# An RWKV-7 layer on one core: the first block's recurrence with the projections' pools kept open for its fillers, its outputs carried through DRAM

## The chip, the cores and the metric

The kernel runs on one core of a Trainium2 chip. The metric is the device time of one execution in microseconds, the median over several runs. A profile of one execution stands beside the times; its engines are named as in the profile: PE is TensorE (PEld its weight loads), DVE is VectorE, ACT is ScalarE, POOL is GpSimd, SP is SyncE, which issues most of the loads.

## What is computed

One layer on a sequence of 2048 tokens of width 1024, in float32: RMS norm, RWKV-7 time mixing with 16 heads of 64, residual, RMS norm, an MLP with squared ReLU and inner width 4096, residual, final RMS norm. The time mixing, cut to what matters here:

```python
xm = x[None] + xx[None] * mu[:, None, None, :]     # token shift, six mixings
rkv = jnp.einsum('nbsd,nde->nbse', xm[:3], w_rkv)  # r, k, v
g = jax.nn.sigmoid(xg @ g1) @ g2                   # gate, inner width 160
def rwkv7_step(state, inp):
    r_t, w_t, k_t, v_t, a_t, b_t = inp
    sa = jnp.einsum('bhvk,bhk->bhv', state, a_t)
    state = (state * w_t[:, :, None, :]
             + sa[..., None] * b_t[:, :, None, :]
             + v_t[..., None] * k_t[:, :, None, :])
    y = jnp.einsum('bhvk,bhk->bhv', state, r_t)
    return state, y
y = group_norm(y) * lnx_w + lnx_b                  # per head
bonus = jnp.sum(r_h * k_h * r_k, axis=-1, keepdims=True) * v_h
y = (y + bonus.reshape(b, s, d)) * g
return y.astype(x.dtype) @ w_o
```

## The kernel before

The sequence is cut into four blocks of 512 tokens. The kernel first runs the projections of all blocks, then the recurrence of block 0, then the rest, in which the output projection and the MLP of block i run while the recurrence of block i+1 is mixed in between. What one part leaves for a later one goes through DRAM: the scores' factors (`d_ar`, `d_bk`), the values `d_v`, the gates `d_g`, the bonus `d_bon` and the normed input `d_hn`.

**Projections.** `r_proj`, `k_proj` and an `epilogue` per block, written for a pool `am` on the right side of SBUF and a pool `ae` on the left; the PSUM pools are `psm` and `pse`. Values and gates are computed here for some blocks only: `v_proj` (L174) for block 0 and block 3, and `g_proj` (L193) for block 0. `g_proj` mixes eight tiles of the input (`mixed`, L143: a ScalarE scaling L157 and a VectorE multiply-add L158), which it reloads from `d_hn` (L170, two buffers `xs`), makes a small product L199 and a large one L209, a selection L211, a sigmoid, splits the gate and its weights into a high and a low part (L84, L85, L220, L228, L229), and runs eight output tiles of four products each (L90 to L92 and L234) whose results ScalarE copies into one of two store buffers `gs` (L236) and GpSimd stores to `d_g` (L237). `v_proj` without parts makes 16 products for each of 2 x 8 weight tiles (L186), and stores through two buffers as well (L190, L191). The eight mixed tiles of g0 take the place of `hn`, the input of the block.

**Recurrence of a block** (`stage_b`, L714): four windows of 128 tokens, each in four chunks of 32. `b_pre` (L558) loads the window's factors (Le, Lo, Bk, ecw, bonw) and makes four groups of score products (L577), which ScalarE copies and VectorE masks (L579 to L581). `b_solve` (L585) puts the scores' triangles into M by a transpose (L588) and solves them on VectorE by 30 steps of a multiply and an add (L595, L596); `b_inv` (L601) spreads the result out into `xbd` (L609). Then the four chunks (`b_chunk`, L611) run one after the other: a product pw, a copy to ws (L639), the product with the solved triangle pu (L642), copies to suv (L643 to L646), a state product pS and the new state. `b_y` (L665) makes the outputs y of the window, and `b_fin` (L676), for the two halves of the heads in turn, loads the values vb and the gates gb of the window (L688, L689), multiplies vb by the bonus (L691, L692), normalises y (L694 to L704), adds vb, multiplies by gb (L705, L706), transposes the result on TensorE (L710) and copies it to the tile `zt` in SBUF (L711), where the output projection of the block finds it. vb and gb have one buffer each.

**What sets the order.** The program is a chain of generators: a main one (projection steps) and a side one (recurrence steps), and after each main step a number of side steps is drawn. The instructions of each engine and of each DMA queue then run in the order that the tile framework's scheduler gives them, with semaphores for data and buffers. A tile pool is a region of SBUF or PSUM. A pool that opens in the space of another waits until what used that space is done, and the instruction that waits holds up what is queued behind it on its engine.

**Block 0's recurrence** has the stretch between the projections and the output projection for itself. Its first ten steps are drawn with nothing between; then `am` and `psm` are closed, pools `zq`, `fp` and `psf` are opened in their place, and as fillers on TensorE the values and gates that are still missing are run, in the order v1, g1, g2, g3, v2, with 1.9 side steps after each filler step (L744 to L762). `fp` has 16 tiles for mixed inputs and six for raw weights. Behind it all three pools are closed, and the pools `bp`, `cp` and `cps` of the last phase are opened in their space: `c_out` (L772) splits the tiles of z and makes the output projection po, `c_norm` the second norm, `c_up` and `c_down` the MLP, with the recurrence of the next block as side steps.

Of the kernel before, what the change touches and what calls it, by code (L numbers as in the profile page):

```python
# [9 lines left out]
F32 = mybir.dt.float32  # L10
# [7 lines left out]
P = 128  # L18
# [21 lines left out]
def trunk(ctx: ExitStack, tc, xt, vecs, lnw, lnb, wr, wk, wv, w1a1, w2, a2,  # L40
# [21 lines left out]

    d_hn = [dram.tile([P, KT, TB + 1], F32, tag=f"d_hn{i}", name=f"d_hn{i}") for i in range(NB)]
# [79 lines left out]
    def mixed(e, hk, vmu, name, parts=True):  # L143

        res = []
        for k in range(KT):
# [3 lines left out]
            elif e.xw:  # L150
                x32 = e.sb.tile([P, TB], F32, tag="x32", name=f"{name}_{k}", bufs=e.xw)
            else:

                if k == 0:
                    xall = e.sb.tile([P, KT, TB + 1], F32, tag="hn", name=f"{name}_all")
                x32 = xall[:, k, 0:TB]
# [17 lines left out]
    def v_proj(e, i, hk, parts=True):  # L174

        xs_ = mixed(e, hk, V_MV, f"xv{i}", parts)
# [16 lines left out]
    def g_proj(e, i, hk):  # L193
        xs_ = mixed(e, hk, V_MG, f"xg{i}", False)
# [311 lines left out]
    run(g_proj(e, 0, reload_hn(e, 0, "g")))  # L506
# [169 lines left out]
    def b_fin(w, r, bp, ps, cfg):  # L676
# [3 lines left out]
        if wd == 0:  # L680

            zts[i] = [(bp if i % 2 else zq).tile([P, 4, TB], F32, tag=f"zh{i % 2}{q}", name=f"zt{i}_{q}") for q in range(2)]
        zt = zts[i]
        for par, y in enumerate(r.y):
# [26 lines left out]
            nc.scalar.copy(zt[par][:, :, wd * WIN:wd * WIN + WIN], pz)  # L711
# [30 lines left out]
    for _ in range(EARLY):  # L742
        next(side)
    pm_.close()  # L744
    zq = ctx.enter_context(tc.tile_pool(name="zq", bufs=1, side="right"))
    with ExitStack() as pf:
        fp = pf.enter_context(tc.tile_pool(name="fp", bufs=1, side="right"))
        psf = pf.enter_context(tc.tile_pool(name="psf", bufs=1, space=PSUM, side="right"))
        FILL = (("v", 1), ("g", 1), ("g", 2), ("g", 3), ("v", 2))
        VS = (None, False, False)  # L750
        e = Env(fp, psf, wb=2, wr=4 if True in VS else 6, xb=8 if True in VS else 1, tb=2, mm=4, xw=8 if True in VS else 16, xs=2)
        BU = 1.9
        acc = 0.0
        for f, i in FILL:
            for _ in (v_proj if f == "v" else g_proj)(e, i, reload_hn(e, i, f), *((VS[i],) if f == "v" else ())):
                acc += BU
                while acc >= 1.0:
                    acc -= 1.0
                    next(side, None)
        for _ in side:  # L760
            pass
    p0.close()  # L762
# [9 lines left out]
    def c_out(i):  # L772

        t0 = i * TB
        zt = zts[i]
        zs = [split(e, zt[k // 4][:, k % 4, :], f"z{i}_{k}") for k in range(KT)]
# [174 lines left out]
```

## Time and profile before

| | |
|---|---|
| time, median of 3 runs | 2986.18 us (2983.82 to 2986.3) |
| the profiled execution | 2978.28 us, span 2976.6 us, mean granted clock 0.978 |
| DMA, mean over the span | 126 GB/s, 373.92 MB |
| last value projection ends | 669.3 us |
| first product with a solved triangle | 735.27 us |
| last y of block 0 starts | 958.12 us |
| first product of the output projection | 1000.0 us |

A row of the trace gives start and length in us, engine, line, operation, output tile <- input tiles, shape, type and the count of instructions that were put together; brackets at its end give the idle time of the engine ahead of it and what ended that. "SPq" is SyncE's queue of DMA issues, "POOLq" that of GpSimd. Rows that group (`by form`) give the busy sum, the mean ns of one, and the idle time ahead of all of them. Matmul ends are modelled by the profiler, so that a sequence of matmuls in one row may overlap the next row a little. The granted clock stands as a share of 2.4 GHz.

### The profile page before, as it was taken

What the parts mean: (1) busy time and instruction counts of PE and PEld (TensorE: products, weight loads), DVE (VectorE), ACT (ScalarE), POOL (GpSimd) and SP (SyncE); (2) the same over time, 40 slices, a digit from 0 to 9 for tenths busy, and PEclk for the clock granted to TensorE, in tenths of its full rate; (3) what the DMA queues carried; (4) which work ended last, traced back from release to release, by engine and by line L of the source; (5) the groups of instructions that cost most, each with busy time, mean ns of one, the idle gap of its engine ahead of it and who ended that gap; (6) DMA issues with size and microseconds to landing.
All of it is one profiled execution on the core that took longest, in us unless ns stands there. A gap on an engine that the chain in (4) does not pass through costs nothing.

```text
span 2976.6 us, 50052 instructions
## 1 busy us (share of the span) xinstructions
PE 2819.1 (95%) x19144; PEld 2129.0 (72%) x19144; DVE 2050.7 (69%) x3858; ACT 1440.7 (48%) x2639; POOL 297.5 (10%) x348
## 2 busy tenths in 40 slices
PE   8999999987989989999998999999899999999998
PEld 5766667754555668777777777778777777878886
DVE  5688888866886577667568767866876786544443
ACT  5667666643474353443534444354445435343342
POOL 0102020131110110000012000001200000110000
PEclk9999999998999999999999999999999999999999
DMA  4444454566563533424343433343333332333332
GB/s 132 152 152 160 152 185 163 169 204 196 152 203 111 155 88 101 114 83 119 98 143 103 112 112 96 110 119 119 110 111 114 93 112 82 113 121 96 92 99 78
DMA packets 192543, 373.92 MB, mean 126 GB/s; under 512 B 41136, under 2 KB 41712, under 8 KB 187696
## 3 DMA queue, kind: packets, MB, share of 16 engines
q1 hardware_dynamic: 175216, 305.49, 34.8%
q0 software_dynamic: 17088, 65.24, 5.8%
q8 instruction: 150, 2.46, 0.4%
q14 instruction: 89, 0.73, 0.1%
HBM read 303.32 MB, written 67.32 MB: 125 GB/s over the span
## 4 chain that ended last, share of the span: by engine, by line
PE 67%; DVE 15%; issue 6%; ACT 5%; DMA 5%; POOL 2%; SPq 0%; ACTq 0%; DVEq 0%; POOLq 0%
PE pd L92 6%; PE pd L91 6%; PE pd L90 6%; PE pu L91 6%; PE pu L90 6%; PE pu L92 5%; DVE tmp L595 2%; DVE M L596 2%; PE pk L90 2%; PE pk L91 2%; PE pk L92 2%; PE po L90 2%; PE po L92 2%; PE po L91 2%; PE pr L90 2%
## 5 line engine op out<-in xcount | busy, mean ns | idle before, releaser
L92 PE MATMUL pd<-uh,d_wl 128*128 128x512 f32 x1024 | 407.2, 398 | 5.9 <-DVE d_wl L85 5.7
L90 PE MATMUL pd<-uh,d_wh 128*128 128x512 f32 x1024 | 405.3, 396 | 0.0
L91 PE MATMUL pd<-ul,d_wh 128*128 128x512 f32 x1024 | 402.6, 393 | 0.0
L84 ACT CAST d_wh<-d_w 128x512 fp32r<-128x512 f32 x256 | 158.6, 621 | 342.9 <-PE pd L91 154.4
L84 ACT CAST u_wh<-u_w 128x512 fp32r<-128x512 f32 x256 | 157.9, 620 | 299.3 <-PE pd L91 116.4
L827 DVE TENSOR_TENSOR h<-h,pd 128x512 f32<-128x512 f32 x256 | 173.9, 681 | 155.7 <-PE pd L92 155.2
L85 DVE TENSOR_TENSOR d_wl<-d_w,d_wh 128x512 fp32r<-128x512 f32 x256 | 179.2, 703 | 120.9 <-ACT d_wh L84 110.7
L85 DVE TENSOR_TENSOR u_wl<-u_w,u_wh 128x512 fp32r<-128x512 f32 x256 | 179.2, 705 | 88.7 <-ACT u_wh L84 78.8
L92 PEld LDWEIGHTS pd<-uh,d_wl 128*128 128x128 f32 x1024 | 192.4, 188 | 56.7 <-DVE d_wl L85 14.9
L91 PEld LDWEIGHTS pd<-ul,d_wh 128*128 128x128 f32 x1024 | 192.5, 188 | 42.4 <-DVE ul L816 0.2
L90 PEld LDWEIGHTS pd<-uh,d_wh 128*128 128x128 f32 x1024 | 192.7, 188 | 39.7 <-ACT uh L815 0.9
L595 DVE TENSOR_TENSOR tmp<-M 96x30 f32<-96x30 f32 (+14 forms) x480 | 158.9, 331 | 19.6 <-POOL M L589 9.2
L596 DVE TENSOR_TENSOR M<-M,tmp 96x30 f32<-96x30 f32 (+14 forms) x480 | 158.3, 330 | 11.2
L816 DVE TENSOR_TENSOR ul<-rl,uh 128x512 fp32r<-128x512 f32 x128 | 88.0, 687 | 73.9 <-ACT uh L815 73.6
L186 PE MATMUL pv<-v,xv 128*128 128x512 f32 x256 | 125.1, 624 | 6.4 <-DVE xv L158 6.1
L577 PEld LDWEIGHTS sc<-Le,Bk 128*64 128x64 f32 x1024 | 67.2, 140 | 45.9 <-issue 34.1
L577 PE MATMUL sc<-Le,Bk 128*64 128x64 f32 x1024 | 77.5, 228 | 17.4 <-DVE Lo L581 7.4
L566 POOL MEMSET Le<- 64x2048 f32 x16 | 28.9, 1804 | 610.5 <-PE y L672 551.5
L642 PEld LDWEIGHTS pu<-ws,xbd 128*128 128x128 f32 x512 | 64.9, 193 | 32.7 <-ACT xbd L609 15.7
L649 PEld LDWEIGHTS pS<-suv,ls 128*64 128x64 f32 x1024 | 65.1, 137 | 32.0 <-ACT suv L646 24.5
L811 ACT ACTIVATE rl<-pu 128x512 f32<-128x512 f32 x128 | 76.0, 594 | 23.2 <-PE pu L92 20.3
L642 PE MATMUL pu<-ws,xbd 128*128 128x64 f32 x512 | 67.7, 275 | 16.2 <-ACT xbd L609 8.3
(695 smaller groups left out, 7241.4 us busy)
## 6 DMA issues: line engine op xcount, KB each, us to landing
u_w<-in_up SPq DMA_DIRECT2D x256, 256.0 KB, 2.7
d_w<-in_down SPq DMA_DIRECT2D x256, 256.0 KB, 2.7
k_w<-in_wk SPq DMA_DIRECT2D x64, 256.0 KB, 2.7
r_w<-in_wr SPq DMA_DIRECT2D x64, 256.0 KB, 2.7
d_ar<-ar POOLq DMA_DIRECT2D x32, 512.0 KB, 3.2
d_bk<-bk POOLq DMA_DIRECT2D x32, 512.0 KB, 3.4
Bk<-d_bk SPq DMA_DIRECT2D x16, 1024.0 KB, 5.1
o_w<-in_wo SPq DMA_DIRECT2D x64, 256.0 KB, 3.1
```

Of the source, the lines that this page charges most:

```text
L84: nc.scalar.copy(hi[0:rows, 0:cols], raw[0:rows, 0:cols])
L85: nc.vector.tensor_tensor(lo[0:rows, 0:cols], raw[0:rows, 0:cols], hi[0:rows, 0:cols], ALU.subtract)
L90: nc.tensor.matmul(out, lhs[0], rhs[0], start=first, stop=False)
L91: nc.tensor.matmul(out, lhs[0], rhs[1], start=False, stop=False)
L92: nc.tensor.matmul(out, lhs[1], rhs[0], start=False, stop=last)
L186: nc.tensor.matmul(pv[tt], xs_[k][:, c], w, start=(k == 0), stop=(k == KT - 1))
L577: nc.tensor.matmul(sc[64:128, p, :], bk[:, p, c, :], Le[:, p, c, :], start=(p == 0), stop=True, skip_group_check=True)
L595: nc.vector.tensor_tensor(tv, M[0:96, s + 1:32, s:s + 1].to_broadcast((96, n, s)), M[0:96, s:s + 1, 0:s].to_broadcast((96, n, s)), ALU.mult)
L596: nc.vector.tensor_tensor(M[0:96, s + 1:32, 0:s], M[0:96, s + 1:32, 0:s], tv, ALU.add)
L642: nc.tensor.matmul(pu[:, k, :], xbd[:, k, c, :], ws[:, k, :], start=(k == 0), stop=True, skip_group_check=True)
L816: nc.vector.tensor_tensor(ul, rl, uh, ALU.subtract)
L827: nc.vector.tensor_add(h[m], h[m], pd)
```

## The change

The pools `am`, `psm` stay open until the recurrence of block 0 is over, and the fillers take their tiles from them: the mixed inputs of the v fillers go into the tag `sh`, those of the gates 1 to 3 into `sl` (ten tiles each), raw weights into the three `wraw` buffers there. The gate of block 0 moves from ahead of the recurrence into the fillers, and the order becomes g0, v1, g1, v2, g2, g3, with 1.6 side steps after each filler step. Since `zq` can't be open beside `am`, block 0's transposed outputs are no longer kept in SBUF: `b_fin` copies each into a tile zw of the tag vb, GpSimd stores it to a new DRAM tensor `d_z`, and `c_out(0)` loads the eight tiles of z back through the tag `t0` (two buffers) ahead of their splits. Blocks 1 to 3 keep zt in SBUF. The diff, without the signature's repeats:

```diff
@@ 60
+    d_z = dram.tile([2, P, 4, TB], F32, tag="d_z", name="d_z")
@@ 143 mixed, v_proj, g_proj
-    def mixed(e, hk, vmu, name, parts=True):
+    def mixed(e, hk, vmu, name, parts=True, tag=None):
-            elif e.xw:
-                x32 = e.sb.tile([P, TB], F32, tag="x32", name=f"{name}_{k}", bufs=e.xw)
+            elif tag:
+                x32 = e.sb.tile([P, TB], F32, tag=tag, name=f"{name}_{k}", bufs=e.xb)
@@ 506
-    run(g_proj(e, 0, reload_hn(e, 0, "g")))
     pe_.close()
@@ 676 b_fin
-        if wd == 0:
+        if wd == 0 and i > 0:
...
-            nc.scalar.copy(zt[par][:, :, wd * WIN:wd * WIN + WIN], pz)
+            if i == 0:
+                zw = bp.tile([P, 4, P], F32, tag="vb", name=f"zw{w}_{par}")
+                nc.scalar.copy(zw, pz)
+                nc.gpsimd.dma_start(d_z[par][:, :, wd * WIN:wd * WIN + WIN], zw)
+            else:
+                nc.scalar.copy(zts[i][par][:, :, wd * WIN:wd * WIN + WIN], pz)
@@ 744
+    BU = 1.6
+    acc = 0.0
+    for f, i in (("g", 0), ("v", 1), ("g", 1), ("v", 2), ("g", 2), ("g", 3)):
+        for _ in (v_proj(e, i, reload_hn(e, i, f), False, "sh") if f == "v" else g_proj(e, i, reload_hn(e, i, f), "sl" if i else None)):
+            acc += BU
+            while acc >= 1.0:
+                acc -= 1.0
+                next(side, None)
+    for _ in side:
+        pass
     pm_.close()
+    p0.close()
     zq = ctx.enter_context(tc.tile_pool(name="zq", bufs=1, side="right"))
-    with ExitStack() as pf:
-        fp = pf.enter_context(tc.tile_pool(name="fp", bufs=1, side="right"))
-        psf = pf.enter_context(tc.tile_pool(name="psf", bufs=1, space=PSUM, side="right"))
-        FILL = (("v", 1), ("g", 1), ("g", 2), ("g", 3), ("v", 2))
...
-    p0.close()
@@ 772 c_out
-        zs = [split(e, zt[k // 4][:, k % 4, :], f"z{i}_{k}") for k in range(KT)]
+        for k in range(KT):
+            if i == 0:
+                z = cp.tile([P, TB], F32, tag="t0", name=f"z{i}_{k}r", bufs=2)
+                nc.sync.dma_start(z, d_z[k // 4][:, k % 4, :])
...
+            zs.append(split(e, z, f"z{i}_{k}"))
```

How the change moves instructions is seen at three places. Line numbers of the changed kernel are up to two off those of the kernel before.

SyncE's queue, where the fillers start: the loads of the first window's values suv, of vb and gb, and of the fillers' first tiles (v_0 and v_1 are tiles of `d_hn`, v_0_0 and v_0_1 raw weights of the value projection, g_0_w and g_1_w and g2t the second weights of gate 0). Before:

```order
L620 DMA suv_5976<-d_v_84 32x512
L621 DMA suv_5977<-d_v_84 32x512
L688 DMA vb_0_7113<-d_v_84 128x512
L689 DMA gb_0_7114<-d_g_92 128x512
L170 DMA v_0_6168<-d_hn_97 128x513
L170 DMA v_1_6173<-d_hn_97 128x513
L164 DMA v_0_0_6212<-in_wv 128x512
L164 DMA v_0_1_6225<-in_wv 128x512
```

and with the change:

```order
L82 DMA g_0_w<-in_g2m 128x512
L227 DMA g2t_0_6114<-in_g2t 32x512 x3
L171 DMA v_0_6258<-d_hn_98 128x513
L171 DMA v_1_6263<-d_hn_98 128x513
L82 DMA g_1_w<-in_g2m 128x512
L620 DMA suv_5806<-d_v_84 32x512
L227 DMA g2t_1_6179<-in_g2t 32x512 x3
L165 DMA v_0_0_6302<-in_wv 128x512
L621 DMA suv_5807<-d_v_84 32x512
```

The two tiles of hn for the value filler now stand ahead of the second half of gate 0's weights, and among them the loads of suv; vb and gb no longer stand there.

VectorE, at the end of the normalisation of a window of block 0 (yc, st, vb, gb), beside the chunks of the next (ws, suv). Before:

```order
L704 TENSOR_TENSOR yc_0_8651<-yc_0_8651,lnwb 128x512
L705 TENSOR_TENSOR yc_0_8651<-yc_0_8651,vb_0_8642 128x512
L643 COPY suv_5972<-pu_0_8431 32x256
L644 COPY suv_5972<-pu_0_8431 32x256
L706 TENSOR_TENSOR yc_0_8651<-yc_0_8651,gb_0_8643 128x512
L691 TENSOR_TENSOR vb_1_8668<-vb_1_8668,bonw_6766 128x512
L692 TENSOR_TENSOR vb_1_8668<-vb_1_8668,lnbb 128x512
```

and with the change:

```order
L700 RECIPROCAL st_1_8408<-st_1_8408 128x8
L702 TENSOR_TENSOR yc_1_8411<-yc_1_8411,st_1_8408 128x512
L703 TENSOR_TENSOR yc_1_8411<-yc_1_8411,lnwb 128x512
L639 COPY ws_1_8210<-pw_1_8193 128x256
L690 TENSOR_TENSOR vb_1_8402<-vb_1_8402,bonw_6722 128x512
L691 TENSOR_TENSOR vb_1_8402<-vb_1_8402,lnbb 128x512
L643 COPY suv_5812<-pu_1_8212 32x256
L644 COPY suv_5812<-pu_1_8212 32x256
```

In both, the multiplication of the second vb by the bonus (L691, now L690) stands among the chunk's copies to ws and suv; it stood behind the first half's last multiplication, and stands now between the second half's normalisation and a copy to suv.

SyncE's queue at the end of the stage, with the first loads of block 1's recurrence (Le, Lo, Bk, ecw, bonw). Before:

```order
L164 DMA v_1_7_8894<-in_wv 128x512
L568 DMA Le_8997<-d_ar_73 64x2048
L569 DMA Lo_8998<-d_ar_73 64x2048
L570 DMA Bk_8999<-d_bk_77 128x2048
L571 DMA ecw_9000<-d_ec_81 128x8x1
L572 DMA bonw_9001<-d_bon_89 128x16
```

and with the change:

```order
L687 DMA vb_1_8530<-d_v_84 128x512
L171 DMA g_2_8756<-d_hn_100 128x513
L165 DMA g_1_8806<-in_g1m 128x512
L171 DMA g_3_8761<-d_hn_100 128x513
L171 DMA g_4_8766<-d_hn_100 128x513
L171 DMA g_5_8771<-d_hn_100 128x513
L171 DMA g_6_8776<-d_hn_100 128x513
L568 DMA Le_9020<-d_ar_73 64x2048
L171 DMA g_7_8781<-d_hn_100 128x513
L82 DMA g_0_w<-in_g2m 128x512
L569 DMA Lo_9021<-d_ar_73 64x2048
```

The loads for gate 3 (g_2 to g_7 are tiles of `d_hn`, g_1 a raw weight) now stand there, and its last tile of hn, g_7, and its second weights stand behind Le.

## Rows read from the trace of the kernel before

**Rows 1.** The page: busy time of each engine over the span.

```profile
PE 2819.1 (95%) x19144; PEld 2129.0 (72%) x19144; DVE 2050.7 (69%) x3858; ACT 1440.7 (48%) x2639; POOL 297.5 (10%) x348
```

**Rows 2.** Stretches: from:to, length, busy us of PE PEld DVE ACT POOL, clock, DMA.

```profile
669.30:735.27 65.97, 50.34 (x313) 26.04 (x312) 43.57 (x94) 24.21 (x41) 7.03 (x13) 0.90 0.64 203
735.27:958.80 223.53, 208.56 (x2400) 121.98 (x2403) 176.75 (x389) 127.19 (x256) 32.63 (x46) 0.98 0.51 156
958.80:1000.00 41.20, 35.18 (x223) 18.45 (x213) 19.59 (x35) 10.41 (x22) 5.76 (x6) 0.90 0.52 153
1000.00:1054.00 54.00, 48.26 (x228) 38.70 (x228) 42.98 (x85) 17.12 (x31) 9.93 (x7) 0.94 0.44 134
```

**Rows 3.** The second window of the recurrence, same columns.

```profile
792.60:866.60 74.00, 66.12 (x736) 39.74 (x732) 63.94 (x140) 50.59 (x98) 14.68 (x20) 1.00 0.66 198
```

**Rows 4.** SyncE's queue where the fillers' pools open: start, length, instruction.

```profile
686.91 0.34 SPq L689 DMA_DIRECT2D gb<-d_g  x1
699.24 0.79 SPq L170 DMA_DIRECT2D v<-d_hn  x2
```

**Rows 5.** TensorE: block 0's gate, a score group, gate products, the first solved chunk.

```profile
669.35 1.93 PE L199 MATMUL pt<-xg_all,g1t 128*32 128x512 f32 x16
671.21 7.14 PE L209 MATMUL pg<-xg_all,g 128*128 128x512 f32 x16
...
679.25 0.27 PE L577 MATMUL sc<-Le,Bk 128*64 128x64 f32 x1
...
680.51 0.50 PE L90 MATMUL pm<-g_wh,sg0h 128*128 128x512 f32 x1
...
682.00 0.39 PE L90 MATMUL pm<-g_wh,sg0h 128*128 128x512 f32 x1
682.23 0.39 PE L91 MATMUL pm<-g_wl,sg0h 128*128 128x512 f32 x1
...
735.27 1.97 PE L642 MATMUL pu<-ws,xbd 128*128 128x64 f32 x8 [5.20 <-ACT xbd L609]
```

**Rows 6.** VectorE: the first window's triangle, transpose in and spread out.

```profile
697.04 1.94 DVE L588 STREAM_TRANSPOSE M<-sy 96x1024 f32<-96x1024 f32 x1
...
733.98 0.85 DVE L609 COPY xbd<-iv 32x512 f32<-32x512 f32 x2
```

**Rows 7.** ScalarE: first and last of the 8 gate copies of block 0.

```profile
683.57 1.07 ACT L236 COPY gs<-pm 128x512 f32<-128x512 f32 x2 [0.46 <-PE pm L234]
...
695.70 0.59 ACT L236 COPY gs<-pm 128x512 f32<-128x512 f32 x1
```

**Rows 8.** VectorE, 669 to 990 us, by form: busy us, mean ns, idle before.

```profile
L158 DVE SCALAR_TENSOR_TENSOR xg<-g,vec,xg 128x512 f32<-128x512 f32 x24 | 17.8, 742 | 3.0 <-ACT xg L157 3.0
...
L85 DVE TENSOR_TENSOR g_wl<-g_w,g_wh 128x512 fp32r<-128x512 f32 x8 | 5.5, 686 | 12.7 <-ACT g_wh L84 12.5
...
L220 DVE TENSOR_TENSOR G<-st,G 32x512 fp32r<-32x512 f32 x4 | 3.7, 918 | 0.1
```

**Rows 9.** DMA issues, 669 to 1000 us: count, KB each, median us to landing.

```profile
d_g<-gs POOLq DMA_DIRECT2D x32, 256.0 KB, 2.7
...
g<-d_hn SPq DMA_DIRECT2D x24, 256.5 KB, 3.3
...
vb<-d_v SPq DMA_DIRECT2D x9, 256.0 KB, 2.9
```

**Rows 10.** TensorE: the last outputs of block 0's recurrence, and the fillers between.

```profile
958.12 1.08 PE L672 MATMUL y<-suv,Lo 128*32 128x64 f32 x57
...
966.68 0.63 PE L710 MATMUL pz<-ident,yc 128*128 128x128 f32 x4 [0.41 <-DVE yc L706]
967.14 7.03 PE L186 MATMUL pv<-v,xv 128*128 128x512 f32 x16
```

**Rows 11.** SyncE's queue at the end of the stage.

```profile
974.74 0.45 SPq L568 DMA_DIRECT2D Le<-d_ar  x1
...
994.71 1.28 SPq L81 DMA_DIRECT2D o_w<-in_wo  x3
```

More of the change, by code (lines that the diff above doesn't have):

```diff
@@ L172, in reload_hn, with v_proj @@
         return hk
-    def v_proj(e, i, hk, parts=True):
-        xs_ = mixed(e, hk, V_MV, f"xv{i}", parts)
+    def v_proj(e, i, hk, parts=True, tag=None):
+        xs_ = mixed(e, hk, V_MV, f"xv{i}", parts, tag)
         for par in range(2):
@@ L191, in v_proj, with g_proj @@
                 nc.gpsimd.dma_start(d_v[i][tt * P:tt * P + P, par, :], vs)
-    def g_proj(e, i, hk):
-        xs_ = mixed(e, hk, V_MG, f"xg{i}", False)
+    def g_proj(e, i, hk, tag=None):
+        xs_ = mixed(e, hk, V_MG, f"xg{i}", False, tag)
         pt = e.ps.tile([P, TB], F32, tag="mm", name=f"pt{i}", bufs=e.mm)
@@ L679, in b_fin @@
         bon = r.bon
-        if wd == 0:
+        if wd == 0 and i > 0:
             zts[i] = [(bp if i % 2 else zq).tile([P, 4, TB], F32, tag=f"zh{i % 2}{q}", name=f"zt{i}_{q}") for q in range(2)]
-        zt = zts[i]
         for par, y in enumerate(r.y):
@@ L743, in trunk @@
         next(side)
+    BU = 1.6
[8 more added lines that the diff above has]
+        pass
     pm_.close()
+    p0.close()
     zq = ctx.enter_context(tc.tile_pool(name="zq", bufs=1, side="right"))
-    with ExitStack() as pf:
-        fp = pf.enter_context(tc.tile_pool(name="fp", bufs=1, side="right"))
-        psf = pf.enter_context(tc.tile_pool(name="psf", bufs=1, space=PSUM, side="right"))
-        FILL = (("v", 1), ("g", 1), ("g", 2), ("g", 3), ("v", 2))
[L750 to L761, printed above, removed]
-    p0.close()
     bp = ctx.enter_context(tc.tile_pool(name="bp", bufs=1))
@@ L774, in c_out @@
         t0 = i * TB
-        zt = zts[i]
-        zs = [split(e, zt[k // 4][:, k % 4, :], f"z{i}_{k}") for k in range(KT)]
+        zs = []
+        for k in range(KT):
+            if i == 0:
+                z = cp.tile([P, TB], F32, tag="t0", name=f"z{i}_{k}r", bufs=2)
+                nc.sync.dma_start(z, d_z[k // 4][:, k % 4, :])
+            else:
+                z = zts[i][k // 4][:, k % 4, :]
+            zs.append(split(e, z, f"z{i}_{k}"))
         hh = [(bp if i % 2 else zq).tile([P, 4, TB], F32, tag=f"zh{i % 2}{q}", name=f"h{i}_{q}") for q in range(2)]
```

## The prediction

> **What bounds the kernel now.** I read the busy line of the page first: TensorE is busy for 95% of the span, VectorE for 69%, ScalarE for 48%, GpSimd for 10% [rows 1]. So time is to be won only where TensorE stands still, or works around something else. The change touches one part of the program, from the end of the last value projection (669.3 us) to the first product of the output projection (1000.0 us), so I cut that part into three stretches with the table of busy time by stretch [rows 2].
>
> In the first stretch (66.0 us, until the first solved chunk of the recurrence) TensorE is busy for 50.3 us, at a mean clock of 0.90: here some 16 us are lost. SyncE's queue shows where. After the load of gb at 686.91 its next instruction, the first load of the fillers, starts at 699.24 [rows 4]: it waits until the old pools are let go, and they are let go when the last gate tile has landed. The first solved chunk starts at 735.27, after an idle time of 5.2 us that a ScalarE copy of the solved triangle ended [rows 5]; the triangle itself entered VectorE at 697.04 and was spread out at 733.98 [rows 6]. So this stretch ends with VectorE's solve, not with TensorE's amount of work.
>
> In the second stretch (223.5 us, four windows of the recurrence with fillers) TensorE is busy for 208.6 and VectorE for 176.8 [rows 2]; in the second window VectorE has 63.9 of 74.0 us [rows 3]. Both engines are near full, and each waits for the other once per chunk. In the third (41.2 us) TensorE has 35.2. It ends with a second wait for pools: the last product of y starts at 958.1 [rows 10], fillers without a dependence run beside and behind it, and the weights of the output projection are asked for only at 994.71 [rows 11]. Ahead of them in the queue, at 974.74, stands Le, the first load into the space of the recurrence's pool.
>
> **The change part by part.** The sum is made against the profiled execution, 2978.28 us, which lies 7.9 us under the median of the runs shown (2986.18); I carry the difference over to the median.
>
> *The first wait for pools goes.* The fillers take tiles of pools that are open already, so nothing waits for the last gate tile; in the new order of SyncE's queue two tiles of hn are asked for ahead of gate 0's second half of weights. Gate 0's products now stand behind and between the score groups of the first window. What must run before the triangle enters VectorE is four score groups (at most 1.26 us each, from 679.25 to 680.51), the small gate product (1.93) and seven eighths of the large one (7.14) [rows 5]: 13 us, and 1.4 for two mask products, so it enters at about 684 instead of 697.0. Against this, by the new order 83 instead of 74 VectorE instructions stand from there to the spread, nine more mixings of 0.74 us [rows 8], or 6.7 us; some 3 us of the old 37.8 were waits for tiles that now come earlier. The first chunk then starts near 725.5 instead of 735.3: **-10 us**. Bounds: -17, where TensorE's own work sets it (48 us of products from 669.3), and -4, where the mixed tiles come late as before, since SyncE has only two tiles of hn and three of raw weights in flight.
>
> *The second stretch gets other fillers.* By the order of the instructions, up to the last y, 30 value products come in and 14 large gate products, 8 small ones, 64 split ones and two selections go out. A value product is two instructions of 0.44 us (16 in 7.03) [rows 10], so 26.4 us come in; the large gate product is 0.89, the small one 0.24, the split one 0.23 [rows 5], a selection about 0.9: some 31 us go out. TensorE has 5 us less. VectorE loses two gates' splittings: six subtractions, four of weights and two of the gate, at 0.69 and 0.92 [rows 8], 8.7 us in all. I take **-7 us**, between 0 and -14.
>
> *Outputs of block 0 go through DRAM.* Eight times the transposed output is copied into a tile of the tag vb, of which there is one, and sent out by GpSimd. The next vb may be loaded only when that has landed. From one transposed output to the next vb in place: transpose 0.63, copy 0.59, two issues 0.8 (0.34 to 0.45 each), out 2.7 like a gate tile, in 2.9 [rows 4, 7, 9, 10, 11]: 7.6 us. Before, this load had no transfer ahead of it. In the new order VectorE has about 4.5 us of its own instructions before it reaches the multiplication by the bonus, and that instruction stands ahead of the copies of the recurrence. So about 3 us of waiting for each of the three windows in the stretch, on the engine that paces it, less what was covered: **+7 us**. Bounds: 0, if the scheduler's other work covers it, and +18, if both halves of each window wait in full. The Trainium skill (DMA: Bandwidth & Descriptors, Anatomy of one DMA) gives a DMA a fixed cost of about 2.0 us, most of it the receipt of the write, and the bytes at 436 GB/s; by an estimate from it a 256 KB tile takes 2.6 us each way, which agrees with the way out and is 0.3 under the way in, and it would make this term 1 us smaller.
>
> *The end becomes a chain of latencies.* Now gates 2 and 3 stand last, and in SyncE's queue the last tile of hn for gate 3 stands behind Le, which waits for the last of the eight transfers. From the last y (959.2 before): normalisation of the first half until its transpose 7.5 (966.68) [rows 10]; trip to the next vb 7.6; four VectorE instructions 2.8; transpose, copy, issue and transfer 4.3; Le issued 0.45 [rows 11]; hn loaded 3.3 with its issue 0.4 [rows 9]; mixed 1.5; the last gate products 1.1. That is 29 us. Then gate 3's own tail, as gate 0 shows it: the large product ended at 678.35, the last of the eight copies at 696.3 [rows 5, 7], 18 us, paced by two store buffers of 2.7 us each and not by TensorE; its transfer 3.2; and from the request for weights to the first product 5.3, as from 994.71 to 1000.0 [rows 2, 11]. Together 55.5 us, where it was 40.8: +15. I add 3 for the 2 MB of Le, Lo and Bk that now share the DMA engines with it: **+18 us**. Bounds: +8, if the copies of gate 2 cover half of the first chain, and +28, if gate 3's products come in one by one and its copies take as long as those of the crowded middle.
>
> *The output projection reads z back.* Four rounds of two tiles, each 2.9 us and two splits, about 4.6 us; one round feeds TensorE for 4 us or more (two tiles by three output tiles by six products of 0.23). So a loss of up to 3 us. On the other side the triangle of the next block can be solved earlier, in a stretch where VectorE has 43.0 of 54.0 us [rows 2]. I put **0**, from -6 to +6.
>
> Sum: -10 - 7 + 7 + 18 + 0 = **+8 us**, so 2986 for the execution profiled, and on the median **2994 us**. A measurement of this kernel can tell about 0.2%, 6 us, from no change.
>
> **The rivals.** *Faster: the trips through vb are covered.* The place is VectorE's multiplication by the bonus. If transfers out and in land within the 4.5 us that VectorE has ahead of it (so 3 us earlier than the medians say), the DRAM term is 0, the second stretch gains 10 because VectorE has less to do, and the chain at the end is 9 and not 18 longer: -10 - 10 + 0 + 9 = -11, or 2975. For it speaks that VectorE idles for 22 us of the first stretch and 47 of the second [rows 2]; against it that the queue is in order, and that GpSimd sends zw behind value tiles which wait for their own store buffers. Chance 0.21.
>
> *No difference: the two waits trade.* The first wait is won, and the chain at the end costs the same 10 to 14 us, since part of it runs beside gate 2's copies and the next triangle is solved in its shade: about 2987. Chance 0.27.
>
> *The change doesn't do what it says.* The fillers still start late: gate 0's eight copies hold the four accumulators until they are stored, and three raw weight buffers instead of six leave the value products waiting. Then the first term is 0: +18, or 3004. For it speaks that the copies of gate 0 took 12 us for eight [rows 7]; against it that the accumulators come free with the copy, not with the landing. Chance 0.10.
>
> **How the numbers follow.** The forecast, 2994, has 0.42. Slower by over 0.2% are most of the forecast and the third rival, 0.50; within it the second rival and the forecast's near edge, 0.28; faster the first rival, 0.22. The range from 2975 to 3009 holds the first rival's time and the third's, and leaves out only where two bounds fall together.
>
> **What would show it.** Right, if SyncE's gap of 12 us after gb is gone, the first solved chunk starts about 56 us after the last value projection and not 66, VectorE's multiplications of vb have waits for DMA of some us, and some 55 us lie between the last y of block 0 and the first product of the output projection. Wrong, if those 55 us are 45 or fewer, or if vb is in place when VectorE comes to it.

## The result, and the profile after

The changed kernel takes 3004.55 us (median of four runs, 3001.4 to 3005.31), the kernel before 2986.24 us beside it: a ratio of 1.0059, 95% interval 1.0042 to 1.0077, or 18 us slower. The profiled execution took 3001.4 us with a span of 2999.3.

TensorE's busy time, on the page of the changed kernel, has grown by 14 us against [rows 1], with the same number of instructions (7.1 of the 14 are the small gate products of gates 1 to 3, below; no other group of products has more than 1.4). The other engines have hardly moved:

```profile
PE 2832.8 (94%) x19144; PEld 2130.7 (71%) x19144; DVE 2055.1 (69%) x3858; ACT 1441.2 (48%) x2639; POOL 301.5 (10%) x356
```

The table of busy time by stretch shows where (columns as in [rows 2]). I cut at the end of the last projected value product, the first product with a solved triangle, the end of the last y of block 0, the first product of the output projection, and the first product of the MLP. The kernel before, with these bounds:

```profile
669.42:735.27 65.85, 50.22 (x312) 25.97 (x312) 43.57 (x94) 24.21 (x41) 6.91 (x13) 0.90 0.64 203
735.27:959.20 223.93, 208.96 (x2409) 122.29 (x2409) 177.15 (x389) 127.19 (x256) 32.63 (x46) 0.98 0.52 156
959.20:1000.01 40.81, 34.78 (x201) 18.14 (x201) 19.20 (x35) 10.42 (x22) 5.76 (x6) 0.90 0.52 150
1000.01:1065.62 65.61, 54.66 (x258) 44.34 (x259) 52.45 (x106) 22.36 (x43) 11.39 (x9) 0.88 0.38 117
```

The changed kernel:

```profile
675.36:737.97 62.61, 51.29 (x316) 25.31 (x316) 44.28 (x96) 25.41 (x43) 7.23 (x13) 1.00 0.68 210
737.97:953.01 215.04, 200.17 (x2357) 114.14 (x2357) 166.65 (x368) 99.70 (x212) 29.75 (x40) 0.99 0.47 141
953.01:1023.09 70.08, 50.81 (x282) 26.52 (x281) 32.29 (x54) 33.55 (x59) 13.69 (x20) 0.85 0.68 195
1023.09:1089.68 66.59, 57.99 (x296) 45.58 (x297) 54.38 (x108) 29.40 (x55) 11.54 (x9) 0.88 0.45 137
```

Start -3.2, middle -8.9, end +29.3, output projection +1.0: together +18.1, close to the difference of the medians (18.3). (The last projected product ends 6 us later in the changed kernel's trace. Most of that is scatter between executions: in the other traces below it ends between 671.4 and 673.3 in the three kernels whose fillers have pools of their own, and between 672.4 and 675.5 in the nine that keep the pools open. Whether some 2 us of it belong to the change is not shown.) So the whole loss, and more, is in the end. It has 16 us more of TensorE work, which the middle no longer has in part (-8.8), and 19.3 us instead of 6.0 in which TensorE stands still.

**The start.** SyncE asks for the fillers' first tiles at 684.61, not at 699.24 [rows 4]: the first wait for pools is gone. The triangle enters VectorE 17.3 us behind the last value product (692.64 - 675.36), where it took 27.6 before [rows 6]. But its solution takes longer: from 692.64 to the spread's end at 737.40 are 44.8 us, where it was 37.8. Timeline of SyncE, VectorE and TensorE in the changed kernel, then VectorE's waits for mixed tiles from 692.6 to 738 us (waited for: us in total, times, longest), then the stretch from the triangle's entry to the spread, before and with the change (columns as in [rows 2]):

```profile
684.61 0.84 SPq L171 DMA_DIRECT2D v<-d_hn  x2
...
692.64 2.00 DVE L588 STREAM_TRANSPOSE M<-sy 96x1024 f32<-96x1024 f32 x1
736.55 0.85 DVE L609 COPY xbd<-iv 32x512 f32<-32x512 f32 x2
...
737.97 1.10 PE L642 MATMUL pu<-ws,xbd 128*128 128x64 f32 x8 [3.56 <-ACT xbd L609]
...
DVE xv L159 <- ACT xv L158: 3.7, 5, 1.9
DVE xg L159 <- ACT xg L158: 1.2, 3, 0.5
...
697.04:734.83 37.79, 26.61 (x86) 12.20 (x86) 31.98 (x77) 10.12 (x15) 1.50 (x3) 0.83 0.62 193
692.64:737.40 44.76, 36.68 (x155) 18.04 (x154) 37.02 (x86) 19.38 (x32) 6.06 (x10) 1.00 0.68 209
```

The same two waits came to 0.9 and 1.4 us before. Of the 7 us that the stretch is longer, 5.0 are work of VectorE (37.0 us for 32.0) and 1.9 idle time. Nine more instructions stand among the steps of the solve, as the prediction counted, but only two of them are mixings (14 for 12); most of the others are gate 0's own splits, and two are the first vb's.

**The middle.** The waits of VectorE for vb grew by 2.3 us (same view, from the first solved chunk to the last y; before, in the changed kernel, and in a kernel that has only the way through DRAM, below):

```profile
DVE vb L691 <- DMA vb<-d_v: 3.2, 2, 1.9
```

```profile
DVE vb L690 <- DMA vb<-d_v: 5.5, 2, 4.8
```

```profile
DVE vb L691 <- DMA vb<-d_v: 3.3, 2, 2.1
```

**The end.** The chain can be read off the timelines of the changed kernel, link by link, from the transpose of the first half to the first output product:

```profile
961.71 0.63 PE L709 MATMUL pz<-ident,yc 128*128 128x128 f32 x4 [2.37 <-DVE yc L705]
966.50 0.34 SPq L687 DMA_DIRECT2D vb<-d_v  x1
970.55 0.69 DVE L690 TENSOR_TENSOR vb<-vb,bonw 128x512 f32<-128x512 f32 x1 [1.17 <-DMA vb<-d_v]
974.41 0.69 DVE L705 TENSOR_TENSOR yc<-yc,gb 128x512 f32<-128x512 f32 x1
974.94 1.91 PE L200 MATMUL pt<-xg,g1t 128*32 128x512 f32 x2 [2.70 <-ACT gs L237]
976.78 1.11 PE L709 MATMUL pz<-ident,yc 128*128 128x128 f32 x4
978.81 0.72 POOL L714 DMA_DIRECT2D d_z<-zw  x1 [2.00 <-ACT zw L713]
981.77 0.45 SPq L568 DMA_DIRECT2D Le<-d_ar  x1
982.32 0.54 SPq L171 DMA_DIRECT2D g<-d_hn  x1
989.77 0.72 ACT L158 ACTIVATE xg<-g,ommu 128x512 f32<-128x512 f32 x1 [5.79 <-DMA g<-d_hn]
992.30 1.12 PE L210 MATMUL pg<-xg,g 128*128 128x512 f32 x2
1013.48 0.58 ACT L237 COPY gs<-pm 128x512 f32<-128x512 f32 x1
1017.03 0.32 SPq L778 DMA_DIRECT2D z_0r<-d_z  x1
1023.09 0.79 PE L91 MATMUL po<-z_0h,o_wh 128*128 128x512 f32 x1 [2.01 <-ACT o_wh L85]
```

From the last y (953.01): 8.7 us to the first half's transpose, 8.8 to the next vb in use, 11.2 until the last zw has landed and Le is asked for, 8.0 until gate 3's last tile, asked for behind Le, is there (7.45 from its request, 3.3 in the median before [rows 9]), 3.7 to the last large product, 20.6 to the last gate copy, 3.0 for its store, 6.1 to the first output product: 70.1. The 11.2 are mostly not a transfer: the second half's outputs are finished on VectorE at 975.10, 4.6 us after vb was there, and then stand behind a small product of gate 3 on TensorE, so that their transposes start only at 976.78. What SyncE waits for ahead of z and the weights is the store of a gate (first row, changed kernel); before it was the store of a value tile (second row), a shorter time:

```profile
SPq L778 <- DMA d_g<-gs: 17.5, 1, 17.5
```

```profile
SPq L81 <- DMA d_v<-vs: 12.9, 1, 12.9
```

The gates' stores land later here than before [rows 9] (DMA issues from 953 to 1023 us: count, KB each, median us to landing):

```profile
d_g<-gs POOLq DMA_DIRECT2D x16, 256.0 KB, 3.7
```

### The profile page after: what moved, and what is told of

It reads as the page before. It is cut to its first block, busy times and chain, and to the rows that moved or that the text cites. A ratio compares the mean times of both kernels' runs of the same rounds, so it can differ in the third digit from the quotient of the medians.

```text
span 2999.3 us, 50109 instructions
## 1 busy us (share of the span) xinstructions
PE 2832.8 (94%) x19144; PEld 2130.7 (71%) x19144; DVE 2055.1 (69%) x3858; ACT 1441.2 (48%) x2639; POOL 301.5 (10%) x356
## 4 chain that ended last, share of the span: by engine, by line
PE 68%; DVE 12%; issue 7%; ACT 5%; DMA 5%; POOL 2%; SPq 0%; DVEq 0%; POOLq 0%; ACTq 0%
PE pd L93 7%; PE pd L91 7%; PE pd L92 7%; PE pu L91 6%; PE pu L92 6%; PE pu L93 6%; PE pk L91 2%; PE pk L92 2%; PE pk L93 2%; DVE M L596 2%; DVE tmp L595 2%; PE pS L649 2%; PE pr L91 1%; PE pr L93 1%; PE pu L642 1%
## 5 line engine op out<-in xcount | busy, mean ns | idle before, releaser
L577 PEld LDWEIGHTS sc<-Le,Bk 128*64 128x64 f32 x1024 | 68.3, 143 | 47.1 <-issue 37.3
L649 PEld LDWEIGHTS pS<-suv,ls 128*64 128x64 f32 x1024 | 65.9, 139 | 31.1 <-ACT suv L646 22.9
L580 DVE TENSOR_TENSOR Le<-sc,mask 64x512 f32<-64x512 f32 x64 | 44.4, 694 | 62.9 <-ACT sy L579 62.2
L642 PEld LDWEIGHTS pu<-ws,xbd 128*128 128x128 f32 x512 | 63.8, 191 | 31.6 <-ACT xbd L609 13.4
```

The source lines that it names most:

```text
L577: nc.tensor.matmul(sc[64:128, p, :], bk[:, p, c, :], Le[:, p, c, :], start=(p == 0), stop=True, skip_group_check=True)
L642: nc.tensor.matmul(pu[:, k, :], xbd[:, k, c, :], ws[:, k, :], start=(k == 0), stop=True, skip_group_check=True)
L649: nc.tensor.matmul(pS[0:64, p, :], lsc[0][:, p, :], S[0][:, p, :], start=(p == 0), stop=True, skip_group_check=True)
```

## The experiments

Each stretch is measured between the same marks as above, in one profiled execution; the ratio to the kernel before comes from repeated runs of both on one chip. Of "end" and "middle" the expectations speak in the same sense.

| | start | middle | end | output proj. | sum | ratio (95%) |
|---|---|---|---|---|---|---|
| before | 65.9 | 223.9 | 40.8 | 65.6 | 396.2 | 1 |
| the change | 62.6 | 215.0 | 70.1 | 66.6 | 414.3 | 1.0059 (1.0042, 1.0077) |
| before_dz | 64.2 | 223.7 | 48.7 | 69.1 | 405.7 | 1.0035 (1.0022, 1.0048) |
| before_dz_zt | 66.0 | 226.5 | 45.0 | 67.1 | 404.6 | 1.0029 (1.0017, 1.0041) |
| zw_hn | 62.6 | 221.1 | 80.3 | 58.2 | 422.2 | 1.0077 (1.0065, 1.0089) |
| v2_last | 63.0 | 245.8 | 42.7 | 72.0 | 423.5 | 1.0100 (1.0083, 1.0116) |
| v2last_bu19 | 62.5 | 242.1 | 52.1 | 66.9 | 423.6 | 1.0091 (1.0076, 1.0106) |
| bu13 | 63.4 | 250.4 | 32.5 | 80.0 | 426.3 | 1.0099 (1.0085, 1.0112) |
| gs_sh | 63.2 | 217.9 | 67.0 | 68.3 | 416.3 | 1.0064 (1.0050, 1.0078) |
| hn_g3 | 63.4 | 219.6 | 61.2 | 67.6 | 411.8 | 1.0055 (1.0039, 1.0072) |
| gs_hn | 62.4 | 218.2 | 62.4 | 70.7 | 413.6 | 1.0061 (1.0045, 1.0076) |
| pt_rev | 62.5 | 222.7 | 74.6 | 59.8 | 419.6 | 1.0052 (1.0037, 1.0066) |
| gs_hn_pt | 62.9 | 228.1 | 55.8 | 66.8 | 413.6 | 1.0028 (1.0017, 1.0040) |
| g0_fp_pt | 56.2 | 230.4 | 63.3 | 66.1 | 416.0 | 1.0053 (1.0039, 1.0067) |

A single profiled sum scatters by some us against the ratio (pt_rev and gs_hn_pt show it, and the profiled execution of v2_last took 10 us more than its median), so verdicts go by the ratio.

**What the way through DRAM costs by itself (before_dz).** The kernel before, with the changed `b_fin` and `c_out` and nothing else:

```diff
+                zw = bp.tile([P, 4, P], F32, tag="vb", name=f"zw{w}_{par}")
+                nc.scalar.copy(zw, pz)
+                nc.gpsimd.dma_start(d_z[par][:, :, wd * WIN:wd * WIN + WIN], zw)
...
+                nc.sync.dma_start(z, d_z[k // 4][:, k % 4, :])
```

> The kernel before (own pools for the fillers, gate 0 ahead, 1.9 steps) with one part of the change alone: block 0's outputs go through the tag vb and DRAM, and the output projection reads them back. Chain theory: VectorE's waits for vb grow from 3.6 to about 8 to 10 us, the end grows by the trip before the last vb and the last store, 41.2 to 50 or 55 us; time 2996 to 3002. If the trips are hidden (rival of the prediction), within 4 us of the kernel before, 2986.

Measured: 2995.71 us, 1.0035, about 10 us. So the way through DRAM is not hidden as a whole. In the middle it is, as the prediction's rival of covered trips said of that place: the middle is unchanged (223.7), and VectorE waits for vb as long as before (3.3 us, shown above). The cost lies in the end and in the output projection, where TensorE works 3.3 us longer than before on one instruction more, at a mean granted clock of 0.82 instead of 0.88 (columns as in [rows 2]):

```profile
961.20:1009.87 48.67, 39.51 (x212) 20.07 (x211) 18.83 (x34) 9.98 (x21) 9.38 (x12) 0.89 0.60 180
1009.87:1079.02 69.15, 57.97 (x259) 46.24 (x259) 54.75 (x109) 26.10 (x49) 11.41 (x9) 0.82 0.33 103
```

**Is it the shared tile? (before_dz_zt, zw_hn).** In the first, the outputs go into the old tiles zt and are stored from there; in the second, on top of the change, into one tile of the tag hn:

```diff
-                zw = bp.tile([P, 4, P], F32, tag="vb", name=f"zw{w}_{par}")
+                zw = zts[i][par][:, :, wd * WIN:wd * WIN + WIN]
```

```diff
+            zts[0] = am.tile([P, KT, TB + 1], F32, tag="hn", name="zall")
...
-                zw = bp.tile([P, 4, P], F32, tag="vb", name=f"zw{w}_{par}")
+                zw = zts[0][:, par * 4:par * 4 + 4, wd * WIN:wd * WIN + WIN]
```

> The kernel before with block 0's outputs stored to DRAM and read back, as in the run that cost 11 us (2995.7), but copied into the SBUF tiles zt as before and stored from there, so that vb is free at once. vb theory (the prediction's term of the trips through vb): the last half's normalisation no longer waits for a store and a load (its vb was asked for at 975.2, 14.0 us after the last y), the last store lands 5 to 8 us sooner, the end falls from 48.7 to 42 to 45 us, time 2988 to 2992. Read-back theory (what costs is that z is asked for with the weights, 6 us ahead of the first product, and after it paces the output projection, and that the last value stores set the pools' release anyway): the end stays at 46 to 50, time 2993 to 2998.

> The changed kernel, but block 0's transposed outputs are copied into one 16 KB tile of the tag hn (free once gate 0's products are done) instead of the tag vb; the stores to DRAM and the reading back stay. Chain theory (the trip out of zw and into the next vb stands on VectorE's path and once more at the end): the 8.3 us that VectorE waited for vb go to under 3, last y of block 0 to first output product falls from 71.0 to about 60 us (8.8 from the first transposed output to vb in place, and some of the normalisation behind it), the time to about 2991 (2987 to 2995). Leftover theory (the end is long because 16 us more of gate products and their copies stand there): the end stays at 68 to 71 and the time within 4 us of the changed kernel's 3004.

Measured: 2993.84 us (1.0029) against 1.0035, intervals that overlap: the end fell to 45.0, but the time, 2993.84, stands at the near edge of what the read-back theory said. By these ratios the shared tile costs about 2 of the 10 us; the intervals leave room for nothing and for some 7, so this is not settled. On top of the change it gives nothing (3007.35, 1.0077), although VectorE's wait for vb in the middle is down to 1.5 us. The end grew to 80.3 us. Six of gate 3's eight tiles of hn now stand behind Le in SyncE's queue, four of them behind Lo too, where it was the last one alone (timeline of SyncE):

```profile
978.73 0.45 SPq L568 DMA_DIRECT2D Le<-d_ar  x1
979.23 1.08 SPq L171 DMA_DIRECT2D g<-d_hn  x2
980.35 0.52 SPq L569 DMA_DIRECT2D Lo<-d_ar  x1
990.35 0.98 SPq L171 DMA_DIRECT2D g<-d_hn  x2
...
998.61 0.85 SPq L171 DMA_DIRECT2D g<-d_hn  x2
```

**Another filler at the end (v2_last, v2last_bu19), or none (bu13).**

```diff
-    for f, i in (("g", 0), ("v", 1), ("g", 1), ("v", 2), ("g", 2), ("g", 3)):
+    for f, i in (("g", 0), ("v", 1), ("g", 1), ("g", 2), ("g", 3), ("v", 2)):
```

v2last_bu19 has this order and BU = 1.9, bu13 the order of the change and BU = 1.3.

> The changed kernel with the fillers in the order g0, v1, g1, g2, g3, v2. Chain theory: value products need no chain of small steps behind them, so the end is set by the normalisation, the vb trip, the last store and the pools' release: 29.6 us as in the changed kernel (952.1 to 981.7), then z and the weights asked for, 6 to the first output product; 38 to 45 instead of 71. TensorE's idle time there falls from 19 to 7 us: the time goes to about 2988 (2980 to 2994). Leftover theory, in which the amount of filler work behind the last y counts and not its kind: about 17 us of products stand there either way, and the time stays at 3000 to 3006.

> The changed kernel with the fillers in the order g0, v1, g1, g2, g3, v2 and 1.9 side steps after each filler step, so that nearly all of v2 is left when the recurrence ends. With 1.6 steps in this order the middle took 245.8 us and the end, 42.7, had only 27.5 us of work to cover a z chain of 32. Expected by the z-chain theory: stretches of about 63, 224, 45 and 69 us up to the first product of the MLP (before: 65.9, 223.9, 40.8, 65.6), so about 5 us over the kernel before, 2990 (2985 to 2996). If the order of the fillers matters in the middle itself (gates beside the recurrence are dear there), the middle stays above 235 and the time above 3000.

> The changed kernel with 1.3 side steps after each filler step instead of 1.6, so that the fillers run out about when the recurrence does. Chain theory: gate 3's chain moves beside the last chunks; the end shrinks to the 30 us of normalisation, vb trip, last store and 8 more, 38 to 48 instead of 71, while the stretch from the first solved chunk to the last y grows by the 16.5 us of products that come in: time about 2992 (2984 to 2998). Leftover theory: what the end loses the middle gains, 3000 to 3008.

Measured: 3013.6, 3013.89 and 3014.46 us. The end did shrink to what the chain theory said (42.7, 52.1, 32.5), but the times fit it nowhere: they lie above both theories' numbers for v2_last and bu13, and where v2last_bu19 was to end up if the order of the fillers matters in the middle itself. The work that left the end made the middle longer by 27 to 35 us, and where nothing is left beside the z chain, TensorE stands still. In bu13 (stretches, columns as in [rows 2]) it works for 6.4 of 32.5 us, its mean granted clock is 0.59 there and 0.80 in the stretch after; the fourth row is the first 15 us of that stretch, and the last one TensorE's wait in the end, for the normalisation of the two halves:

```profile
736.18:986.53 250.35, 236.57 (x2455) 133.07 (x2455) 179.76 (x385) 123.98 (x251) 34.58 (x50) 0.97 0.48 146
986.53:1019.04 32.51, 6.36 (x24) 4.21 (x24) 14.07 (x27) 9.23 (x16) 8.28 (x10) 0.59 0.65 213
1019.04:1099.08 80.04, 66.18 (x387) 49.99 (x387) 59.82 (x116) 27.61 (x52) 11.18 (x9) 0.80 0.43 123
...
1019.04:1034.00 14.96, 12.02 (x47) 6.51 (x49) 4.53 (x8) 3.70 (x6) 0.00 (x0) 0.50 0.88 232
...
PE pz L709 <- DVE yc L705: 15.6, 2, 10.8
```

So the z chain alone is 32.5 us. Against the change, bu13's end is 37.6 us shorter and its middle 35.3 longer, since 36.4 us of TensorE's work moved there: that is nearly even. What it loses stands in the output projection, 13.4 us longer, whose first 15 us run at the lower clock (in the change about the first 5). An end without fillers beside it was not cheaper.

**Which link of the end's chain? (gs_sh, hn_g3, gs_hn, pt_rev, gs_hn_pt).** Three edits of gates 2 and 3, alone and together: more store buffers, gate 3's input loaded into the free tile hn, and the small products in one row:

```diff
-                gs = e.sb.tile([P, 512], F32, tag="vs", name=f"gs{i}_{par}_{tt}", bufs=2)
+                gs = e.sb.tile([P, 512], F32, tag="sh" if i > 1 else "vs", name=f"gs{i}_{par}_{tt}", bufs=e.xb if i > 1 else 2)
```

```diff
+        if name == "g" and i == 3:
+            h3 = e.sb.tile([P, KT, TB + 1], F32, tag="hn", name="h3")
...
+                nc.sync.dma_start(h3[:, k, :], d_hn[i][:, k, :])
+                return h3[:, k, :]
```

```diff
-        for k in range(KT):
+        for k in reversed(range(KT)):
...
-xs_[k], start=(k < 4), stop=(k >= 4),
+xs_[k], start=(k >= 4), stop=(k < 4),
```

> The changed kernel, but the gate copies of gates 2 and 3 take store buffers of the tag sh (ten, free behind v2) instead of the two of vs. After the first four runs two theories of the long end are left. Gate-chain theory: the end (70.1 us from the last y to the first output product) is set by gates 2 and 3 themselves, of which the eight copies of each take 15 to 16 us because a store must land before a buffer is free. Then the end falls to 56 to 62 us and the time to about 2994 (2989 to 2998). Loads theory: the end is set by gate 3's tiles of hn, which come two by two and the last behind block 1's Le; then the copies of gate 2 are not what it waits for, gate 3's own copies give 6 us, and the time is 2998 to 3003.

> The changed kernel, but the eight tiles of hn for gate 3 are loaded into the 16 KB tile hn (free once gate 0's products are done) and not through the two buffers xs. Loads theory: gate 3's mixing (last one 991.3 in the changed kernel) is done by about 970, its products follow gate 2's, the end falls from 70 to 52 to 58 us, the time to 2988 to 2994. Gate-chain theory: the copies of gate 2 (to 981) and then of gate 3 through two buffers stay; the end falls by 3 to 8, the time to 2997 to 3003.

> Both edits together. If both chains bound the end in turn, it falls to what TensorE has to do there (50.8 us of work at a granted clock of 0.85, about 45 at full clock) or to the 30 us of the z chain and 6 more: 46 to 55 us, time 2981 to 2990. If something else sets it (block 1's 2 MB of Le, Lo and Bk on the DMA engines, which all these kernels have), it stays over 60 and the time over 2993.

> The changed kernel, but the eight small gate products of a gate (L200) are written in reverse order of the mixed tiles, so that the last tile to come starts them and they stand in one row. In the trace of the changed kernel eight in a row took 1.93 us (gate 0), but where single ones stand between large gate products each takes about 1.04; the four gates have 16.0 us of them, the kernel before 8.9. Work theory: TensorE's time counts there, the 16.0 fall to about 9, the stretches from the last value product to the first product of the MLP lose 5 to 7 us, time 2998 (2995 to 3000). Wait theory: the end is set by tiles and stores that come late, the products only fill it; then idle time takes the place and the time is 3002 to 3006.

> The same edit on top of the one with ten store buffers for gates 2 and 3 and gate 3's input in the tile hn (3001.7, small gate products 13.9 us there). Work theory: 13.9 to 9, and since both waits are taken away already all of it shows: 2995 (2992 to 2999). Wait theory: 3000 to 3004.

Measured: 3005.8, 3003.04, 3001.74, 3002.75 and 2994.6 us. No edit alone, nor the first two together, can be told from the change (1.0052 to 1.0064 against 1.0059). gs_sh missed both theories' numbers, hn_g3 stands at the edge of where the gate copies keep the bound, gs_hn where neither chain sets it, pt_rev where waits do. All three together give 1.0028, what the work theory said with both waits away, and half of the loss back. That would fit links of which each, once shortened, is covered by another, but no trace shows it: the last step, gs_hn to gs_hn_pt, takes 4.4 us of small products away (12.0 to 7.6), the ratios differ by about 10 us, and the four stretches of the two profiled executions have the same sum. That the small products matter at all is in TensorE's rows by form (busy us, mean ns | idle before): 48 instructions took 7.0 us before and 14.1 with the change. In the first fence is the row of before, in the second that of the change with gate 0's eight in a row (16 instructions) and one that stands alone in the end:

```profile
L199 PE MATMUL pt<-xg,g1t 128*32 128x512 f32 x48 | 7.0, 599 | 0.0
```

```profile
L200 PE MATMUL pt<-xg,g1t 128*32 128x512 f32 x48 | 14.1, 622 | 5.1 <-ACT gs L237 2.7 <-DVE xg L159 1.5 <-DMA g1t<-in_g1t 0.9
...
676.37 1.93 PE L200 MATMUL pt<-xg_all,g1t 128*32 128x512 f32 x16
984.83 1.04 PE L200 MATMUL pt<-xg,g1t 128*32 128x512 f32 x2
```

pt_rev took 6.5 of those 7 us of work away (14.1 to 7.6) and won nothing that can be told; the products now wait for the last tile: in its end, and then in that of gs_hn_pt, where the tiles come sooner:

```profile
L200 PE MATMUL pt<-xg,g1t 128*32 128x512 f32 x16 | 3.6, 1060 | 11.7 <-DVE xg L159 11.7
```

```profile
L205 PE MATMUL pt<-xg,g1t 128*32 128x512 f32 x16 | 3.6, 1060 | 3.5 <-DVE xg L159 3.5
```

**Gate 0 as a filler without the rest (g0_fp_pt).** The kernel before, z in SBUF, with the small products reversed as above and

```diff
-    run(g_proj(e, 0, reload_hn(e, 0, "g")))
...
-        FILL = (("v", 1), ("g", 1), ("g", 2), ("g", 3), ("v", 2))
+        FILL = (("g", 0), ("v", 1), ("g", 1), ("g", 2), ("g", 3), ("v", 2))
```

> The kernel before with its own pools for the fillers and z kept in SBUF, but gate 0 taken from ahead of the recurrence to the head of the fillers, as the change does, and the small gate products in one row. It keeps the part of the change that gained and leaves out the way through DRAM. If the first stretch's gain comes from gate 0 as a filler, first stretch 62 to 64 us (65.9 before), middle 217 to 224, end and output projection as before (41 and 66): 2980 (2976 to 2984) against 2985. If it comes from the pools that stay open (no wait for the last stores of the projections), the first stretch stays at 66 or grows, because all fillers still wait for the new pools, now without gate 0's products ahead: 2986 to 2996.

Measured: 3002.57 us, 1.0053, slower than either theory said. The first stretch shrank by 9.7 us, but 20 us of TensorE work left it, and as much stands in the end now (54.9 us of work, 34.8 before), which is 22.5 us longer; the middle has 6.5 more. The fillers still waited for the new pools, until 679.85 (stretches, then SyncE's timeline):

```profile
671.39:727.55 56.16, 29.68 (x249) 18.01 (x249) 44.99 (x96) 22.84 (x38) 4.00 (x7) 0.67 0.55 169
957.97:1021.25 63.28, 54.91 (x249) 26.41 (x248) 19.29 (x35) 12.84 (x26) 7.91 (x10) 0.97 0.46 138
...
679.85 0.82 SPq L170 DMA_DIRECT2D g<-d_hn  x2
```

None of these versions beats the kernel before.

## Why the prediction was right, and where its terms were off

The sign, the place and the range held: slower, by a chain at the end, with 3004.55 between 2975 and 3009. The size did not: 8 us were forecast and 18 measured, because two terms were mis-sized and one was put in the wrong place. That the range held is partly luck: the start and the end together came out 18 us dearer than forecast, and the middle, with its two terms, 9 us cheaper (-8.9 for 0). Without that the time would have been near 3013.

- **"The first wait for pools goes": -10 us forecast, -3.2 measured.** The wait is gone, and the triangle enters VectorE 10.3 us sooner behind the last value product, where 13 were reckoned (684 for 697.0). The step that failed most is "some 3 us of the old 37.8 were waits for tiles that now come earlier": VectorE's waits for mixed tiles grew from 2.3 to 4.9 us, and the solve with all that stands among it from 37.8 to 44.8 us, where 41.5 were reckoned (37.8 - 3 + 6.7). The first solved chunk came 62.6 us after the last value product, not about 56. The bound named for it, mixed tiles that come late, was the case, and a little worse than its edge of -4.
- **"The second stretch gets other fillers": -7 us forecast.** The middle lost 8.9 us; TensorE's work there fell by 8.8 and VectorE's by 10.5. The term was about right, if the trips through vb cost nothing there.
- **"Outputs of block 0 go through DRAM": +7 us in the middle.** Wrong in place, near in size. VectorE's waits for vb in the middle grew by 2.3 us with the change and by 0.1 in before_dz. The way through DRAM costs 8 to 11 us (1.0029, 1.0035) when it is the only edit: behind the last y in before_dz, and for 2.6 us in the middle in before_dz_zt. Whether the tile that zw shares with vb is part of the cost is not settled.
- **"The end becomes a chain of latencies": +18 us forecast, +29.3 measured.** The links were the right ones, in the right order: 55.5 us were reckoned for the chain and 70.1 passed. Only the last store was shorter than reckoned (3.0 for 3.2); all others were longer. The largest are the last zw behind the vb (11.2 for 7.1), gate 3's last tile behind Le (8.0 for 4.2) and the gate copies (20.6 for 18). The step that failed is to price links that run beside each other by the rows of calmer stretches. For gate 3's tile and the gate copies the transfers are slower: Le, Lo and Bk, the gates' stores and the trips of z share the DMA engines there (0.68 of their time busy, 0.52 before), and the stores of gates take 3.7 us in the median, not 2.7 [rows 9]. For the last zw it is the engines: from vb in use to zw copied are 8.0 us where 4.0 were reckoned, behind mixings and products of gate 3, and its store takes about as long as reckoned. Small products that stand singly, 8.2 us in this stretch instead of 2 for a gate in one row, were not in the sum. And a sum of links is no proof that each one bounds: taking one out alone gave nothing.
- **"The output projection reads z back": 0 forecast, +1.0 measured** with the change. In before_dz the same reading has +3.5 in that stretch, inside the bound. One figure of the term doesn't come out as written: two tiles by three output tiles by six products of 0.23 are 8.3 us; with the three products that `mm3` makes they are the 4 us of the text.

The rival "the change doesn't do what it says" had the right time, 3004, by the wrong way: its fillers that still start late did not occur. The rival "the trips are covered" was right about the middle, where VectorE hardly waited longer for vb, and fell with the end, 29 us longer where it said 9; "the two waits trade" fell with the end's 70 us as well.

The estimate from the Trainium skill (DMA: Bandwidth & Descriptors, Anatomy of one DMA), 2.6 us for 256 KB, is too low for the crowded stretch, where the measurement decides: the tile of hn behind Le took 7.45 us from request to use, and z's eight tiles have 3.0 to 4.6 us to landing. The page gives its fit for DMAs that GpSimd issues, so it bears on the stores; the prediction put SyncE's loads under it too.

What is shown: the way through DRAM costs about half as much by itself, in the kernel before, as the whole change, and the three edits together give half of the loss back. What is only argued: that these are the two halves, since no run has both. Why gates in the middle lengthen it so much (v2_last), and where gs_hn_pt wins its time, was not taken apart.

## What to carry to other kernels

Filler work at the end of a serial stretch has to end sooner than the chain that it covers: a projection with small steps, splits and eight paced stores behind it becomes part of the chain itself. Products whose results only need storing shortened the end here, but not the time, since what they replaced went into a stretch that was nearly full. Before moving such work, sum its own tail from its request to its last store, with the latencies of the stretch into which it comes. Where several chains meet at one wait (here the release of pools), an experiment that shortens one of them says little; shortening all and putting them back one by one, which was not done here, would say more.

## What the runs showed of the hardware

Eight small products that fill a quarter of TensorE's columns each took 1.93 us in one row (0.24 each) but 1.04 us when a large product stood between two of them, as long as a large one (1.12): here they overlapped only with each other. The scheduler had split them as their inputs arrived, and 7 us of TensorE work came with that.

TensorE's granted clock fell where it had waited: in bu13's end it is 0.59 in the mean, with waits of 15.6 us for the normalisation, and it is 0.50 for the first 15 us of the output projection behind it. In the ends of pt_rev and gs_hn_pt the small products that follow waits of 11.7 and 3.5 us show 1060 ns each, against 599 in the kernel before. Of gs_hn_pt, the stretch ahead of these products and that of the products (columns as in [rows 2]):

```profile
984.00:987.70 3.70, 0.31 (x3) 0.07 (x1) 2.93 (x5) 2.62 (x5) 1.86 (x4) 0.62 0.85 291
987.70:991.40 3.70, 3.64 (x17) 0.66 (x17) 0.01 (x1) 0.00 (x0) 2.99 (x2) 0.50 0.75 200
```

A clock of 0.50 is the lower of TensorE's two levels, 1.2 GHz against 2.4. So a gap cost more there than its own length: 3.64 us for what takes 1.93 at full clock.
